# Nine convolution taps a tile by ScalarE and adding transfers, and two gate tiles taken out of a merge pair, in a hybrid decoder layer

## The chip, the cores and the metric

The kernel runs on one core of a Trainium2 chip, as one program in one launch. The metric is the device time of one execution in microseconds (us). The engines are named as the profile names them: PE is the matrix engine (TensorE), PEld its weight loads, DVE is VectorE, ACT is ScalarE, POOL is GpSimd, SP is the engine that issues most loads. DMA transfers issued from POOL can add what they carry onto what lies at their destination ("adding" or accumulating transfers); those from SP only copy.

## The reference

One layer over 512 tokens of 1,024 channels, all in float32. After a norm, one wide projection feeds two mixers that run side by side. Their outputs are gated, added and projected; a feed-forward block follows. Cut to what matters here:

```python
u = _rmsnorm(h, norm1_g[l])
proj = u @ w_in[l]
a_glu, q, k, v, r, g_low, gate_a, gate_b = _split_cols(proj)

c = a_glu[..., :CONV_CH] * jax.nn.sigmoid(a_glu[..., CONV_CH:])
c = _causal_dwconv(c, conv_dw_w[l], conv_dw_b[l])      # 31 taps for each channel
c = jax.nn.silu(_layernorm(c, conv_ln_g[l], conv_ln_b[l]))
y_conv = c @ w_conv_out[l]
...
o = _gla_chunked(qh, kh, vh, gkh)                      # 4 heads, chunks of 64 tokens
o = o * lax.rsqrt(jnp.mean(o * o, axis=-1, keepdims=True) + EPS) * gla_norm_g[l]
o = o.reshape(bsz, seq, GLA_VDIM) * jax.nn.silu(r)
y_gla = o @ w_gla_out[l]

merged = jax.nn.sigmoid(gate_a) * y_conv + jax.nn.sigmoid(gate_b) * y_gla
h = h + merged @ w_o[l]
u2 = _rmsnorm(h, norm2_g[l])
z = _causal_dwconv(u2 @ w_ffn_up[l], ffn_dw_w[l], ffn_dw_b[l])
h = h + (jax.nn.silu(z[..., :FFN_DIM]) * z[..., FFN_DIM:]) @ w_ffn_down[l]
```

## The kernel before

**Matrix products.** Each float32 operand is split into a high part, rounded to PE's reduced float32, and a low part, the rest. A product is three matmuls (`mm3`, L471: high by low, low by high, high by high). A weight tile is 128 by 1,024 values, 512 KB. `split_weight` (L368) makes the parts: ACT casts the high part (L380, L410); the low part comes from a DVE subtraction (L381, L415), or, for tiles in `ADDED` (L46), from a negated copy by ACT (L412) onto which a transfer from POOL adds the weight once more (L413). A plain tile (`col_tile`, L479) is 24 matmuls of 512 columns. `two_tiles` (L1211) computes two tiles together by seven products instead of eight, as 84 matmuls of 256 columns, with four weight splits, of sums that POOL adds up, and some combining operations.

**The stages.** (1) The first norm and half of v. (2) The glu tiles: for each of eight channel tiles one product for the gate, whose sigmoid ACT makes (L846), and one for the value, which DVE multiplies in (L850). (3) The low-rank decay (`w_low`), the other half of v (four accumulator banks at once, L501), the four heads' decays. (4) The heads: for each, queries, keys, scores, states and outputs, with other tiles between so that PE has work while DVE prepares. Three of the eight glu pairs stand here (`LATE_GLU`, L39), and after the last head four gb tiles (gate B), `AHEAD` of them. (5) `w_r`, the gate r, by a seven-product scheme over pairs. (6) The merge: six pairs of gate tiles (`MERGE`, L37), with the tiles of `w_gla` and `w_conv` between them (`BEHIND`). (7) `w_o` and the feed-forward block.

**The depthwise convolution.** It runs on DVE as background work. `conv_chain` (L801) turns a channel tile's 31 taps into two half-length sequences, 16 offsets with three operations each: one into the first half of `conv[k]`, one into its second half with the tap sums and x0 + x1 (L807), one into the tile's half of `aside`. Offset 0 is three activations on ACT (L811); offsets 1 to 15 are 44 operations on DVE (L815), each multiplying by a tap and adding; three closing operations follow (L829, L831, L833). When all eight tiles are through, `add_up` (L863) sums them for the layer norm's mean, and `norm_chain` does the rest.

**What sets the order.** Every use of a weight tile calls `weight` (L433), which prefetches the splits of the next two tiles and then calls `fill` (L455) with a share of work: `fill` pops operations from the first chain in `chains`, each costing 0.6 of room, until the room is used up. So the taps are dealt out along the weight tiles by a rate written by hand (`RATE`, the shares at L438). A new chain is appended by each glu pair (L851). The remaining order within an engine is made when the program is built and is fixed from then on: each engine runs its instructions strictly in that order, and waits at each for the semaphores that it needs. The buffers that matter: 5 PSUM banks `mm` and 3 `ax`, taken in turn; 4 raw weight tiles, 4 high and 4 low parts; 26 `h` tiles; `btmp` has 2 buffers, and one of them holds the tap sums as long as the convolution runs; `tmp` has 6.

Of the kernel before, what the change touches and what calls it, by code (L numbers as in the profile page):

```python
# [21 lines left out]
KT = D // P  # L22
# [12 lines left out]
AHEAD = 4  # L35

MERGE = [("w_gb", 4, 5), ("w_gb", 6, 7), ("w_ga", 0, 1), ("w_ga", 2, 3), ("w_ga", 4, 5), ("w_ga", 6, 7)]  # L37
R_PAIRS = ((0, 4), (1, 5), (2, 6), (3, 7))
LATE_GLU = 3  # L39
_HALVES = [("w_gla", 2 + h // 2, h % 2) for h in range(12)]  # L40
BEHIND = [[], _HALVES[:4], _HALVES[4:8], _HALVES[8:]]
BEHIND += [[("w_conv", m, half) for m in pair for half in range(2)] for pair in O_PAIRS[:2]]
MERGE_REST = [("w_conv", m) for pair in O_PAIRS[2:] for m in pair]
LOOK = 2
# [3 lines left out]
RATE = 5.0  # L48
WARM = (6, 1, 2, 2)
# [25 lines left out]
PP_N = PP_FB + 2 * FT  # L75


@with_exitstack
def trunk_layer(ctx: ExitStack, tc: tile.TileContext, a: dict, out: bass.AP):
# [139 lines left out]
    for h in range(HEADS):  # L219
        order += [("w_qk", 2 * h), ("w_qk", 2 * h + 1)]  # L220
        if h:
            order += glu_order[KT - LATE_GLU + h - 1]
# [4 lines left out]
    for (name, p, q), behind in zip(MERGE, BEHIND):  # L227
# [3 lines left out]
        if not behind:  # L231
            order += [("w_gla", 0), ("w_gla", 1)]
# [200 lines left out]
    def weight(name, j, ahead=LOOK):  # L433
# [5 lines left out]
        if name == "w_qk":  # L439
            share = 1.0 if j < 2 else RATE + 1.0  # L440

# [5 lines left out]
    room = [0.0]  # L447
    after, urgent, hold, conv_given = [], [], [True], []
# [5 lines left out]

    def fill(n):  # L455
        room[0] += n
        while (urgent or chains) and room[0] > 0:
            chain = urgent or chains[0]
            share, work = chain.pop(0)
# [5 lines left out]
            if chains and not chains[0]:  # L465
                chains.pop(0)
                start_chain()
# [333 lines left out]
    def conv_chain(k, c):  # L801
# [33 lines left out]
        chain = [(0.6, begin)]  # L835
        for j in range(ET_):
            for i in range(3 if j < OT_ else 2):
                chain.append((0.6 if j else 0, lambda j=j, i=i: list(parts(j))[i]()))
        return chain + [(0.6, lambda n=n: finish(n)) for n in range(3)]
# [295 lines left out]
    gbs = {}  # L1135

    def gate_b(m):
        gbs[m] = col_tile(weight("w_gb", m), acts1)
# [133 lines left out]
    for h in range(HEADS + 1):  # L1272
        old = heads[h - 1] if h else None
        new = heads[h] if h < HEADS else None
        if new:
            late_glu = glu(KT - LATE_GLU + h - 1)
            new.decays()
            new.queries()
        else:
            gate_b(0)  # L1280
# [4 lines left out]
        new.keys() if new else gate_b(1)  # L1285
        if old:
            old.states()
            next(late_glu) if new else gate_b(2)
            old.outputs()
            next(late_glu) if new else gate_b(3)  # L1290
# [6 lines left out]
    part = [None] * KT  # L1297
    gas = {}

    def sigmoid(m, acc):  # L1300
        g = heap()
        nc.scalar.activation(g, acc, AF.Sigmoid)
        return g
# [20 lines left out]

    for m in range(AHEAD):
        part[m] = sigmoid(m, gbs.pop(m))
# [118 lines left out]
    def pair_7(n):  # L1445
# [5 lines left out]
        for j in range(4):  # L1451
# [11 lines left out]
            if j == 0 or n >= 3:  # L1463
# [3 lines left out]
            if j == 3:  # L1467
# [7 lines left out]
                if n >= 3:  # L1475
# [15 lines left out]
    for n in range(4):  # L1491
# [384 lines left out]
```

## Time and profile before

| | us |
|---|---|
| median of 3 runs | 832.7 |
| the runs | 832.09, 832.7, 836.29 |
| the profiled execution | 833.33 |
| its span in the trace | 831.6 |

PE's granted clock in the profiled execution is 0.996 of full speed. A profile's page gives busy time by engine, and groups of instructions by source line ("L815 DVE ... x120 | 57.0, 475": 120 instructions, 57.0 us busy in all, 475 ns for one). "Waits" lists who waited for whom. A view by stretches gives the busy time of each engine between two times, and a timeline gives single instructions: start, duration, engine, line, output and inputs, and in brackets the idle time before it and what ended it. Instructions on one engine overlap at their ends, so the distance of starts tells what one costs, and a duration alone tells more than that. Transfers are listed with their size and the median time from issue to landing.

### The profile page before, as it was taken

To read this page: it belongs to the slowest core of one execution; us is meant where nothing else is said; L and a number is where in the kernel's file an instruction comes from. 1 tells how busy PE (TensorE), PEld (TensorE's weight loads), DVE (VectorE), ACT (ScalarE), POOL (GpSimd) and SP (SyncE) were. 2 spreads that over 40 slices of the span, in tenths; PEclk is the share of its full clock that TensorE was granted. 3 is DMA by queue.
4 is the path that set the end of the run, shared out by engine and by line. 5 is a ranking of instruction groups with operands and counts; after the bars stand their busy time and mean duration, and the time that the engine had idled before them with its cause. 6 is when DMAs were issued, how large, how long until landed. Compare 5 with 4: busy or idle time off the path is not lost.

```text
span 831.6 us, 11495 instructions
## 1 busy us (share of the span) xinstructions
PE 811.6 (98%) x4263; PEld 696.9 (84%) x4263; DVE 725.3 (87%) x1166; ACT 464.1 (56%) x688; POOL 167.9 (20%) x149
## 2 busy tenths in 40 slices
PE   9999999999989898999999999999999999999996
PEld 7888888887877777999988898899889988899885
DVE  6789999999998998676778889989974999789895
ACT  6654685746545544485444546556444663456654
POOL 2011111211122333323000200221122301522012
PEclk9999999999999999999999999999999999999999
DMA  8497868468213122334448633046643356334662
GB/s 327 141 200 180 233 148 199 107 157 201 52 50 96 63 96 76 102 102 153 129 125 227 178 102 102 26 130 176 144 133 102 107 172 151 116 102 164 166 127 101
DMA packets 36473, 113.60 MB, mean 137 GB/s; under 512 B 3689, under 2 KB 8945, under 8 KB 36417
## 3 DMA queue, kind: packets, MB, share of 16 engines
q1 hardware_dynamic: 28912, 86.39, 30.2%
q0 software_dynamic: 7488, 26.48, 18.6%
q8 instruction: 33, 0.54, 0.3%
q14 instruction: 24, 0.19, 0.1%
q10 hardware_dynamic: 16, 0.00, 0.0%
HBM read 110.76 MB, written 2.10 MB: 136 GB/s over the span
## 4 chain that ended last, share of the span: by engine, by line
PE 84%; DVE 10%; issue 3%; ACT 1%; DMA 0%; POOL 0%; POOLq 0%; DVEq 0%; ACTq 0%; SPq 0%
PE mm L475 24%; PE mm L476 24%; PE mm L477 24%; PE mm L689 3%; DVE wlo L381 2%; PE ax L477 2%; PE ax L476 2%; PE ax L475 2%; DVE c L815 2%; DVE aside L815 1%; DVE tmpq L1174 1%; DVE h L1431 1%; DVE wlo L415 1%; DVE btmp L869 1%; DVE kept L328 1%
## 5 line engine op out<-in xcount | busy, mean ns | idle before, releaser
L475 PE MATMUL mm<-uh,wlo 128*128 128x512 f32 (+1 forms) x608 | 219.7, 361 | 0.0
L476 PE MATMUL mm<-ul,whi 128*128 128x512 f32 (+1 forms) x608 | 217.5, 358 | 0.0
L477 PE MATMUL mm<-uh,whi 128*128 128x512 f32 (+1 forms) x608 | 217.2, 357 | 0.0
L477 PEld LDWEIGHTS mm<-uh,whi 128*128 128x128 f32 x608 | 114.8, 189 | 16.9
L475 PEld LDWEIGHTS mm<-uh,wlo 128*128 128x128 f32 x608 | 114.9, 189 | 16.7 <-issue 0.2
L476 PEld LDWEIGHTS mm<-ul,whi 128*128 128x128 f32 x608 | 114.9, 189 | 16.2
L381 DVE TENSOR_TENSOR wlo<-raw,whi 128x1024 fp32r<-128x1024 f32 x86 | 100.7, 1176 | 31.9 <-ACT whi L380 28.0
L352 POOL TENSOR_TENSOR raw<-raw,raw 128x512 f32<-128x512 f32 x42 | 65.1, 1551 | 249.3 <-DVE wlo L381 139.7
L380 ACT CAST whi<-raw 128x1024 fp32r<-128x1024 f32 x86 | 82.7, 964 | 38.3 <-PE mm L477 31.7
L410 ACT CAST whi<-raw 128x1024 fp32r<-128x1024 f32 x78 | 81.4, 1047 | 28.5 <-PE mm L477 13.1
L415 DVE TENSOR_TENSOR wlo<-raw,whi 128x1024 fp32r<-128x1024 f32 x50 | 66.6, 1336 | 7.6 <-ACT whi L410 7.3
L380 ACT CAST whi<-kept 128x1024 fp32r<-128x1024 f32 (+1 forms) x40 | 40.2, 1008 | 39.8 <-DVE kept L328 23.4
L815 DVE SCALAR_TENSOR_TENSOR c<-h,pp,c 128x255 f32<-128x255 f32 (+14 forms) x120 | 57.0, 475 | 1.6 <-ACT c L811 1.5
L815 DVE SCALAR_TENSOR_TENSOR c<-aside,btmp,c 128x255 f32<-128x255 f32 (+14 forms) x120 | 57.0, 475 | 0.0
L815 DVE SCALAR_TENSOR_TENSOR aside<-h,pp,aside 128x255 f32<-128x255 f32 (+6 forms) x112 | 53.2, 475 | 0.0
L381 DVE TENSOR_TENSOR wlo<-kept,whi 128x1024 fp32r<-128x1024 f32 (+1 forms) x40 | 47.8, 1195 | 5.0 <-ACT whi L380 4.9
L412 ACT ACTIVATE wlo<-raw 128x1024 fp32r<-128x1024 f32 x28 | 29.6, 1058 | 38.4 <-PE mm L475 29.4
L1600 DVE SCALAR_TENSOR_TENSOR tmp<-mm,pp,tmp 128x511 f32<-128x511 f32 (+1 forms) x56 | 41.3, 740 | 4.0 <-ACT tmp L1597 3.9
L1218 ACT COPY tmp<-mm 128x256 f32<-128x256 f32 x48 | 17.7, 368 | 43.7 <-PE mm L477 43.2
L1379 DVE TENSOR_TENSOR hres<-hres,mm 128x512 f32<-128x512 f32 (+1 forms) x49 | 32.2, 668 | 3.3 <-PE mm L477 2.4
L1597 ACT ACTIVATE tmp<-mm,pp 128x512 f32<-128x512 f32 x28 | 21.8, 777 | 19.1 <-PE mm L477 18.9
L352 POOL TENSOR_TENSOR raw<-raw 128x512 f32<-128x512 f32 x14 | 28.7, 2049 | 0.0
(383 smaller groups left out, 1902.9 us busy)
## 6 DMA issues: line engine op xcount, KB each, us to landing
raw<-in_w_up_dram SPq DMA_DIRECT2D x44, 512.0 KB, 3.6
raw<-in_w_glu_dram SPq DMA_DIRECT2D x16, 512.0 KB, 5.4
raw<-in_w_down_dram SPq DMA_DIRECT2D x15, 512.0 KB, 4.1
wlo<-in_w_glu_dram POOLq DMA_DIRECT2D x12, 512.0 KB, 6.8
kept<-in_w_down_dram POOLq DMA_DIRECT2D x10, 512.0 KB, 5.5
raw<-in_w_v_dram SPq DMA_DIRECT2D x8, 512.0 KB, 7.0
raw<-in_w_qk_dram SPq DMA_DIRECT2D x8, 512.0 KB, 7.2
wlo<-in_w_qk_dram POOLq DMA_DIRECT2D x8, 512.0 KB, 8.6
```

The source lines that it names most:

```text
L352: work = nc.gpsimd.tensor_tensor(out, x, y, ALU.add)
L380: nc.scalar.copy(hi, raw)
L381: two_low[:] = [nc.vector.tensor_tensor(lo, raw, hi.bitcast(F32), ALU.subtract)]
L410: nc.scalar.copy(hi, raw)
L412: pace[0] = nc.scalar.mul(lo, raw, -1.0)
L415: pace[0] = nc.vector.tensor_tensor(lo, raw, hi.bitcast(F32), ALU.subtract)
L475: nc.tensor.matmul(acc, ll, rh, start=first, stop=False, **kw)
L476: nc.tensor.matmul(acc, lh, rl, start=False, stop=False, **kw)
L477: nc.tensor.matmul(acc, lh, rh, start=False, stop=last, **kw)
L815: nc.vector.scalar_tensor_tensor(out[:, j:], x[:, : half_t - j], w, out[:, j:], ALU.mult, ALU.add)
L1379: done = nc.vector.tensor_tensor(hres[t, n][:, c], hres[t, n][:, c], acc[:, c], op)
L1600: nc.vector.scalar_tensor_tensor(z[:, s:], acc[:, : T - s], w[j], z[:, s:], ALU.mult, ALU.add)
```

## The change

1. `Taps`, a new kind of chain: its first three offsets (1, 2 and 3; tile 0 has none) can be done ahead by ACT and two adding transfers, as `added(j)`: three activations make the three products of an offset, two of them into one `btmp` tile and one into a `tmp` tile; then one transfer adds the `btmp` tile onto both halves of `conv[k]`, another the `tmp` tile onto `aside`. Each seventh time that `fill` takes an operation from the first chain, the second chain in the list starts its next one (`run_ahead`): first its offset 0, then an offset each time. What has not been started by the time that a chain comes to the front is done by DVE as before (`begin`).
2. `LATE_GLU` is 2: six glu pairs run in a row, two between the heads. In the place of the third stand two gb tiles; after the last head come four more. `AHEAD` is 6, and the pair gb 4 and 5 leaves `MERGE`.
3. `w_gla` tiles 6 and 7 are plain tiles behind the third pair, which had been halves behind the fourth; the sigmoids of gb tiles are taken at once; shares for the last gb tiles.

In the program as built, tile 1 has two offsets done ahead, tiles 2 to 5 have three each, tiles 6 and 7 none: 14 offsets, 42 operations that leave DVE, 42 activations and 28 transfers that come.

```diff
--- before.py
+++ after.py
@@ -32,20 +32,23 @@
 EPS = 1e-6
 O_PAIRS = ((0, 2), (1, 3), (4, 6), (5, 7))
 GROUPS = (((0, 2), (1, 3), (4, 6), (5, 7)), ((8, 10), (9, 11), (20, 21)), ((12, 14), (13, 15), (16, 18), (17, 19)))
-AHEAD = 4
-
-MERGE = [("w_gb", 4, 5), ("w_gb", 6, 7), ("w_ga", 0, 1), ("w_ga", 2, 3), ("w_ga", 4, 5), ("w_ga", 6, 7)]
+AHEAD = 6
+
+MERGE = [("w_gb", 6, 7), ("w_ga", 0, 1), ("w_ga", 2, 3), ("w_ga", 4, 5), ("w_ga", 6, 7)]
 R_PAIRS = ((0, 4), (1, 5), (2, 6), (3, 7))
-LATE_GLU = 3
-_HALVES = [("w_gla", 2 + h // 2, h % 2) for h in range(12)]
-BEHIND = [[], _HALVES[:4], _HALVES[4:8], _HALVES[8:]]
+LATE_GLU = 2
+_HALVES = [("w_gla", 2 + h // 2, h % 2) for h in range(8)]
+BEHIND = [[], _HALVES[:4], _HALVES[4:8]]
 BEHIND += [[("w_conv", m, half) for m in pair for half in range(2)] for pair in O_PAIRS[:2]]
 MERGE_REST = [("w_conv", m) for pair in O_PAIRS[2:] for m in pair]
+PLAIN_GLA = {0: (0, 1), 2: (6, 7)}
 LOOK = 2
 ADDED = {("w_glu", j) for j in range(4, 2 * KT)} | {("w_qk", m) for m in range(KT)}
 ADDED |= {("w_v", KT // 2 + j) for j in range(KT // 2)} | {("w_gb", m) for m in range(AHEAD)}
 RATE = 5.0
+TAPS_AHEAD = 3
+AHEAD_EVERY = 7
 WARM = (6, 1, 2, 2)
 MID = 4
 EARLY = 2
@@ -73,6 +76,21 @@
 PP_FW = PP_GG + DV // P
 PP_FB = PP_FW + 2 * FT * FW
 PP_N = PP_FB + 2 * FT
+
+
+class Taps(list):
+
+    def __init__(self, ahead, rest, taps):
+        super().__init__(rest)
+        self.ahead, self.taps = ahead, taps
+
+    def begin(self):
+        if self.ahead:
+            if len(self.ahead) == len(self.taps) + 1:
+                self.ahead.pop(0)()
+            at = len(self.taps) - len(self.ahead)
+            self[:0] = sum(self.taps[at:], [])
+            self.ahead = []
 @with_exitstack
@@ -218,18 +236,18 @@
     order += [("w_v", KT // 2 + j) for j in range(KT // 2)]
     for h in range(HEADS):
         order += [("w_qk", 2 * h), ("w_qk", 2 * h + 1)]
-        if h:
+        if 0 < h <= LATE_GLU:
             order += glu_order[KT - LATE_GLU + h - 1]
     order += [("w_gb", m) for m in range(AHEAD)]
     order += [("w_r", (R_PAIRS, step, d)) for step, d in R_STEPS]
     tight = set()
     first = len(order)
-    for (name, p, q), behind in zip(MERGE, BEHIND):
+    for n_pair, ((name, p, q), behind) in enumerate(zip(MERGE, BEHIND)):
         for n, part in enumerate(("x1", "x3", "x2", "x4")):
             order.append(("two", (name, p, q, part)))
             order += [tile[:2] for tile in behind[n : n + 1] if tile[2] == 0]
-        if not behind:
-            order += [("w_gla", 0), ("w_gla", 1)]
+        if n_pair in PLAIN_GLA:
+            order += [("w_gla", m) for m in PLAIN_GLA[n_pair]]
     tight |= set(range(first, len(order)))
     order += MERGE_REST
     order += [("w_o", (O_PAIRS, step, d)) for step, d in STEPS]
@@ -438,6 +456,8 @@
         share = {"two": 2.5, "w_glu": RATE + 0.75, "w_r": 2.0}.get(name, RATE)
         if name == "w_qk":
             share = 1.0 if j < 2 else RATE + 1.0
+        if name == "w_gb" and j > 3:
+            share = 2.0 if j == 4 else 6.8
         fill(share + (1.75 if order[min(len(ready), len(order)) - 1] in ADDED else 0))
         return ready[used[0] - 1]
@@ -445,17 +465,28 @@
     chains = []
     room = [0.0]
+    turn = [0]
     after, urgent, hold, conv_given = [], [], [True], []
     behind = []
     def start_chain():
         if not chains and after and conv_given == KT * [1] and not (hold and len(after) == 1):
             chains.append(after.pop()())
+
+    def run_ahead(chain):
+
+        turn[0] += 1
+        follower = chains[1] if len(chains) > 1 else None
+        if follower and follower.ahead and turn[0] % AHEAD_EVERY == 1:
+            follower.ahead.pop(0)()
     def fill(n):
         room[0] += n
         while (urgent or chains) and room[0] > 0:
             chain = urgent or chains[0]
+            if not urgent and isinstance(chain, Taps):
+                chain.begin()
+                run_ahead(chain)
             share, work = chain.pop(0)
             room[0] -= share
             with ExitStack() as order_of:
@@ -464,6 +495,7 @@
                 work()
             if chains and not chains[0]:
                 chains.pop(0)
+                turn[0] = 0
                 start_chain()
         if not chains and not urgent:
             room[0] = 0.0
@@ -832,11 +864,34 @@
             if n == 2:
                 nc.vector.tensor_tensor(y0[:, 1:], y0[:, 1:], other[:, : half_t - 1], ALU.add)
-        chain = [(0.6, begin)]
-        for j in range(ET_):
-            for i in range(3 if j < OT_ else 2):
-                chain.append((0.6 if j else 0, lambda j=j, i=i: list(parts(j))[i]()))
-        return chain + [(0.6, lambda n=n: finish(n)) for n in range(3)]
+        def start():
+            begin()
+            for part in parts(0):
+                part()
+
+        def added(j):
+
+            at = PP_CW + k * CW + CW - 1 - 2 * j
+            both = btmp().rearrange("p (two n) -> p two n", two=2)[:, :, : half_t - j]
+            odd = tmp(half_t)[:, : half_t - j]
+            src = slice(0, half_t - j)
+            for out, x, w in (
+                (both[:, 0], x0, pp[:, at : at + 1]),
+                (both[:, 1], xs, taps[:, k, j : j + 1]),
+                (odd, x1, pp[:, at - 1 : at]),
+            ):
+                nc.scalar.activation(out, x[:, src], AF.Copy, scale=w)
+            y = conv[k].rearrange("p (two n) -> p two n", two=2)[:, :, j:]
+            nc.gpsimd.dma_start(y, both, accum_op=ALU.add)
+            nc.gpsimd.dma_start(other[:, j:], odd, accum_op=ALU.add)
+
+        def by_dve(j):
+            return [(0.6, lambda i=i: list(parts(j))[i]()) for i in range(3 if j < OT_ else 2)]
+
+        ahead = range(1, 1 + TAPS_AHEAD if k else 1)
+        rest = sum((by_dve(j) for j in range(1, ET_) if j not in ahead), [])
+        rest += [(0.6, lambda n=n: finish(n)) for n in range(3)]
+        return Taps([start] + [lambda j=j: added(j) for j in ahead], rest, [by_dve(j) for j in ahead])
     sum_taps()
@@ -1132,10 +1187,15 @@
         low_at[:] = [nc.vector.scalar_tensor_tensor(lo, po, gain, hi.bitcast(F32), ALU.mult, ALU.subtract)]
         oa[m] = hi, lo
-    gbs = {}
+    part = [None] * KT
+
+    def sigmoid(m, acc):
+        g = heap()
+        nc.scalar.activation(g, acc, AF.Sigmoid)
+        return g
     def gate_b(m):
-        gbs[m] = col_tile(weight("w_gb", m), acts1)
+        part[m] = sigmoid(m, col_tile(weight("w_gb", m), acts1))
     H = T // 2
@@ -1273,34 +1333,28 @@
         old = heads[h - 1] if h else None
         new = heads[h] if h < HEADS else None
         if new:
-            late_glu = glu(KT - LATE_GLU + h - 1)
+            late_glu = glu(KT - LATE_GLU + h - 1) if h <= LATE_GLU else None
             new.decays()
             new.queries()
         else:
-            gate_b(0)
+            gate_b(2)
         if old:
             old.scores()
         if not new:
             urgent += s1_n2[:3] + of_s1 + s1_n2[3:] + of_n2
-        new.keys() if new else gate_b(1)
+        new.keys() if new else gate_b(3)
         if old:
             old.states()
-            next(late_glu) if new else gate_b(2)
+            next(late_glu) if h <= LATE_GLU else gate_b(0 if new else 4)
             old.outputs()
-            next(late_glu) if new else gate_b(3)
+            next(late_glu) if h <= LATE_GLU else gate_b(1 if new else 5)
     behind += [roots_at[0]]
     gla_scope.close()
     late_scope, late = scoped("late", 1, "right")
     r_scope, rp_ = scoped("r", 8, "right")
-    part = [None] * KT
     gas = {}
-
-    def sigmoid(m, acc):
-        g = heap()
-        nc.scalar.activation(g, acc, AF.Sigmoid)
-        return g
     def gla_out(m, py):
         nc.vector.tensor_tensor(part[m], py, part[m], ALU.mult)
@@ -1322,8 +1376,6 @@
             outs[name][1](m, acc[1])
         return acc
-    for m in range(AHEAD):
-        part[m] = sigmoid(m, gbs.pop(m))
     def seven(name, pairs, acts, complete, at=lambda step, i: None, fine=False, put=None, before=lambda step: None):
@@ -1460,7 +1512,7 @@
                     gated_o(m, ax_bank)
                 if j == 2:
                     start_norms()
-            if j == 0 or n >= 3:
+            if j == 0 or n >= 2:
                 while complete_pairs:
                     complete_pairs.pop(0)()
@@ -1472,7 +1524,7 @@
                         (part if name == "w_gb" else gas)[m] = sigmoid(m, c)
                 complete_pairs.append(sigmoids)
-                if n >= 3:
+                if n >= 2:
                     complete_pairs.pop()()
             for proj, m, half in behind[j : j + 1]:
                 open_tiles[proj, m] = tile_of(proj, m, half_of[half], open_tiles.get((proj, m)))
@@ -1488,17 +1540,16 @@
         hold.clear()
         start_chain()
-    for n in range(4):
+    for n in range(3):
         pair_7(n)
-        if n == 0:
-            for m in range(2):
-                tile_of("w_gla", m, range(KT))
+        for m in PLAIN_GLA.get(n, ()):
+            tile_of("w_gla", m, range(KT))
     def merged(m):
         if m not in merged_tiles:
             j = [m in p for p in O_PAIRS].index(True)
             if j < 2:
-                pair_7(4 + j)
+                pair_7(3 + j)
             else:
                 tile_of("w_conv", m, range(KT))
         return merged_tiles[m]
```

## The prediction

> **What bounds the kernel now.** I read the page's busy times first, then the waits of TensorE (PE), then busy time by stretch.
>
> ```profile
> span 831.6 us, 11495 instructions
> PE 811.6 (98%) x4263; PEld 696.9 (84%) x4263; DVE 725.3 (87%) x1166; ACT 464.1 (56%) x688; POOL 167.9 (20%) x149
> ```
>
> PE is short of the span by 20.0 us. No change that leaves PE's work alone can win more than that and whatever PE runs at a lower clock. The waits say where it is lost (us in total, times, longest):
>
> ```profile
> PE mm L475 <- DVE r L1429: 2.4, 1, 2.4
> PE ax L476 <- DVE wlo L381: 2.3, 1, 2.3
> PE mm L476 <- DVE wlo L381: 1.8, 2, 1.2
> PE mm L475 <- DVE wlo L415: 1.4, 2, 0.7
> PE ax L897 <- ACT sum L928: 1.2, 1, 1.2
> PE ax L897 <- DVE sum L929: 1.2, 1, 1.2
> PE ax L1124 <- DVE h L1132: 0.8, 1, 0.8
> ```
>
> All seven hang on VectorE (DVE) or on what stands just behind it; together 11.1 us. The stretches place them (stretch: length, then busy PE, weight loads, DVE, ScalarE (ACT), GpSimd (POOL), PE clock, DMA share, GB/s):
>
> ```profile
> 60.00:215.00 155.00, 154.80 (x704) 128.10 (x703) 152.04 (x372) 96.38 (x150) 25.68 (x28) 1.00 0.70 169
> 240.00:260.00 20.00, 15.86 (x68) 12.15 (x67) 20.00 (x29) 12.75 (x18) 6.93 (x4) 1.00 0.08 27
> 260.00:280.00 20.00, 17.57 (x78) 14.27 (x77) 17.36 (x19) 9.91 (x13) 5.11 (x3) 1.00 0.44 133
> 280.00:300.00 20.00, 18.39 (x136) 16.79 (x134) 20.00 (x37) 11.37 (x19) 1.38 (x1) 1.00 0.31 105
> 300.00:320.00 20.00, 17.06 (x76) 13.74 (x77) 19.64 (x23) 8.87 (x12) 7.60 (x4) 0.91 0.27 89
> 215.00:320.00 105.00, 93.77 (x461) 76.91 (x460) 101.60 (x146) 55.37 (x87) 24.00 (x14) 0.98 0.27 82
> 320.00:475.00 155.00, 155.00 (x878) 136.47 (x877) 115.79 (x156) 81.44 (x121) 33.63 (x25) 1.00 0.47 138
> ```
>
> From 240 to 320 us PE is idle 4.14 + 2.43 + 1.61 + 2.94 = 11.1 us: the same 11.1. That is the w_r product and the first merge pair, and DVE is full there (101.6 of 105). From 60 to 215 us (glu, w_v, the heads) DVE is full too, 152.0 of 155, and PE does not wait yet: the two are level. Behind 320 us PE never waits. One more loss shows in the clock of 0.91 after the last wait:
>
> ```profile
> 317.39 0.63 PE L476 MATMUL mm<-oa,whi 128*128 128x512 f32 x1
> 317.82 0.63 PE L477 MATMUL mm<-oa,whi 128*128 128x512 f32 x1
> ...
> 91.14 0.39 PE L475 MATMUL mm<-whi,ul 128*128 128x512 f32 x1
> ...
> 93.86 0.39 PE L475 MATMUL mm<-whi,ul 128*128 128x512 f32 x1
> ...
> 347.16 0.28 PE L476 MATMUL mm<-hq,whi 128*128 128x256 f32 x1
> 347.28 0.28 PE L477 MATMUL mm<-sumsq,whi 128*128 128x256 f32 x1
> ```
>
> Starts of 512-column matmuls are 0.43 us apart there, against 0.227 at 91 us (twelve steps in 2.72); the clock of 0.91 over 20 us says 1.8 us lost, and I count 1.6 (eight matmuls, 0.2 each). So 12.7 us hang on a late DVE behind 240 us.
>
> **The change, part by part.** *Matmuls.* Two gb tiles become plain tiles instead of a pair of seven products. By the changed order 84 matmuls of 256 columns go (x 0.12, the last pair of rows, = 10.1 us) and 48 of 512 come (x 0.227 = 10.9): +0.8 us of PE.
>
> *DVE behind 240 us.* In the changed order every tap of the last tile, and all additions of `add_up`, stand ahead of `of_s1`'s subtraction (L1187); before, 44 taps and these stood behind it.
>
> ```profile
> 87.76 0.47 DVE L815 SCALAR_TENSOR_TENSOR c<-aside,btmp,c 128x254 f32<-128x254 f32 x1
> 88.15 0.46 DVE L815 SCALAR_TENSOR_TENSOR aside<-h,pp,aside 128x254 f32<-128x254 f32 x1
> ...
> 89.34 1.11 DVE L850 TENSOR_TENSOR h<-mm,tmp 128x512 f32<-128x512 f32 x1
> ...
> L869 DVE TENSOR_TENSOR btmp<-btmp,c 128x512 f32<-128x512 f32 x6 | 6.2, 1030 | 0.1
> L866 DVE TENSOR_TENSOR btmp<-c,c 128x512 f32<-128x512 f32 x1 | 1.1, 1121 | 0.0
> ```
>
> A tap follows the last after 0.39 us: 44 are 17.2 us, `add_up` 7.3, the three closing operations 1.1. The gb pair's four splits and three combines go as well (about 5). From 215 to 320 us that is 31 of 101.6, and the 70 left are well under PE's 93.8. I let the waits go except the 0.8 at L1124, which stands directly behind w_r's last product, a real dependency: -11.9 us. If all goes it is -12.7.
>
> *DVE ahead of it.* The 25.6 us just named move into the glu and head stretch, less 42 taps that ScalarE takes over (14 offsets of three, for tiles 1 to 5: 16.4 us): +9.2 us of DVE there, against 10.9 more of PE (the two gb tiles) and 3.0 of idle DVE. Level again, with 4.7 to spare. Tiles 6 and 7 have nobody ahead of them and keep all their taps.
>
> *The new waits.* An offset now costs three activations, then two accumulating transfers from POOL, and of `btmp`'s two buffers one holds the tap sums throughout. So the next offset's first activation into `btmp` waits in ACT's own order until the last transfer has landed, and everything behind it on ACT waits too: weight casts, the negated copies, glu's sigmoids. POOL's second transfer into `aside` also waits for the first, ahead of weight transfers. And DVE can start the next tile only when its last offset has landed.
>
> ```profile
> 43.73 1.06 ACT L412 ACTIVATE wlo<-raw 128x1024 fp32r<-128x1024 f32 x1 [1.53 <-PE mm L475]
> 45.10 0.87 POOL L413 DMA_DIRECT2D wlo<-in_w_glu_dram  x1 [4.37 <-ACT wlo L412]
> ...
> 57.30 0.60 ACT L811 ACTIVATE c<-h,pp 128x256 f32<-128x256 f32 x1 [0.69 <-DVE h L850]
> 57.81 0.49 ACT L811 ACTIVATE aside<-h,pp 128x256 f32<-128x256 f32 x1
> ...
> wlo<-in_w_glu_dram POOLq DMA_DIRECT2D x12, 512.0 KB, 6.8
> wlo<-in_w_qk_dram POOLq DMA_DIRECT2D x8, 512.0 KB, 8.6
> raw<-in_w_down_dram POOLq DMA_DIRECT2D x5, 512.0 KB, 5.3
> raw<-in_w_down_dram POOLq DMA_DIRECT2D x1, 256.0 KB, 3.6
> ```
>
> One round t: two activations (1.0), from ACT's end to POOL's issue 0.3 (44.79 to 45.10), and the landing of 255 KB. Landing: from below 3.6 (256 KB of such a transfer, no load); from above 6.8 (512 KB among the glu loads). Halving saves 1.7 (5.3 to 3.6), so 5.1 under load. I take 4.6, nearer to the loaded row because the DMA share is 0.70 here: t = 5.9, with ends of 4.9 and 8.1. The other thing that would add, smaller pieces (1,020 bytes a row instead of 4,096), no row shows.
>
> Rounds against the DVE work that covers them, counted in the changed order from a tile's x0 + x1 (L807) to its first own tap into c: tile 1, two rounds, 18 taps, a glu product (1.1), three closing operations = 9.2 us; tile 2, three rounds, 32 taps and the same = 14.7; tile 3, three rounds, 35 taps, a glu product and small work = 16.8; tiles 4 and 5, three rounds, 20 and 22, because the gate's and the first head's operations stand between. Nothing before this slows DVE, so its lateness adds up to 8t - 40.7. What is late next is glu's sixth product (L850), which frees the fourth accumulator bank of w_v. Before, the last such product ended at 90.45 (89.34 + 1.11) and PE wanted the bank nine matmuls after w_v's first at 91.14, at 93.2: 2.7 to spare. In the changed order 23 more taps, a product and four small operations (11.5 us) stand ahead of it against two more glu tiles (10.9), so 2.1 are left. PE's wait = 8t - 42.8: at 5.9, **4.4 us**; at 4.9 nothing; at 8.1, 22.
>
> ACT's 42 activations (23 us at 0.55) and POOL's 28 issues (24 at 0.87) fit: ACT has 58 us and POOL 129 free from 60 to 215. The load order on SP changes by two gb tiles only and stays ahead. Behind 320 us one merge pair fewer stands between the layer norm and its use; DVE has 39 us of idle time there to cover it, so nothing.
>
> The Trainium skill ("DMA: Bandwidth & Descriptors", Anatomy of one DMA) puts a GpSimd transfer at 2.0 us plus bytes over 436 GB/s, an estimate of 2.6 for 255 KB; t would be 3.9 and the sum that of the first rival. Its 3.2 for 512 KB stands against 5.3 and 6.8 here, so I don't follow it.
>
> **Sum**, against the profiled execution (833.33 us with what lies around its 831.6 of span; the median of the runs shown is 0.6 lower): 833.3 - 11.9 + 0.8 + 4.4 = 826.6; against the median **826 us**.
>
> **Rivals.**
> *All landings are hidden* (t under 5.35). For it: the unloaded row. Against it: the DMA share of 0.70. 833.3 - 11.9 + 0.8 - 0.6 = 822 us.
>
> *The landings chain becomes the bound, and it is slower.* Place: ACT waiting for `btmp` in the glu stretch, seen by PE at w_low and w_v. It takes back the whole gain when 8t - 42.8 passes 11.1, at t = 6.7. Price: landing 5.1, activations 1.0, hand-over 0.3, one other transfer's issue in front 0.9: t = 7.3; 8t - 42.8 = 15.6, and tile 4 adds 3t - 20 = 1.9: 833.3 - 11.9 + 0.8 + 17.5 - 0.6 = 839 us. For it: qk's 8.6 to land. Against it: the loaded rows are of 512 KB, twice the size, and the unloaded one lands in 3.6. By the Trainium skill ("TensorE: Matmul & The Clock Gate", Part 1) PE drops to half clock after an idle window of some 3.4 us, which would put about 2 more on such a wait; the rows at 317 us show half speed after two waits of 1.2.
>
> *The change doesn't do what it says:* w_r's waits stay, because they hang on loads and not on taps.
>
> ```profile
> L328 DVE TENSOR_TENSOR kept<-kept,raw 128x1024 f32<-128x1024 f32 x6 | 7.8, 1302 | 2.5 <-DMA raw<-in_w_r_dram 2.5
> ```
>
> Then 2.4 + 2.3 + 1.8 remain: 833.3 - 5.4 + 0.8 + 4.4 - 0.6 = 832.5 us. Against it: DVE was busy 20.0 of 20 where PE lost most.
>
> **How the numbers follow.** Forecast 0.33, hidden 0.27, slower 0.27, doing nothing 0.13. Half a per cent, about what a measurement here can tell, is 4.2 us. Faster (under 828.5): all of hidden and three quarters of the forecast, 0.52. Slower (over 836.9): most of the slower rival, 0.26. Between: 0.22. The range must reach both: from 818 (hidden, with the last 0.8 and some of the rest of PE's small losses gone) to 840 (the slower rival); the forecast's own is 822 to 831.
>
> **What would show it.** Right: no taps behind L1187's first row and PE near 100% from w_r to the layer norm's mean; PE 0.8 us busier in matmuls; a PE gap of 2 to 8 us at w_low or w_v, with ACT waiting for a transfer out of `btmp`. Wrong: no gap there (822), a gap over 11 us or a second one at the heads (839), or PE still waiting for L381 or L1429 in w_r (832.5).

## The result and the profile after

| | before | after |
|---|---|---|
| median, us | 833.09 (4 runs, 832.09 to 836.29) | 876.55 (4 runs, 875.08 to 877.57) |
| ratio | | 1.0513, 95% interval 1.0481 to 1.0546 |
| span of the profiled execution | 831.6 | 874.6 |
| PE busy in it | 811.6 | 825.2 |
| span less PE busy | 20.0 | 49.4 |

The changed kernel is 43.5 us slower. Line numbers are now those of the changed kernel: L475 has become L507, L815 L847, L807 L839, L850 L905, L413 L431, L1429 L1481; new are the activations of L883 and the two adding transfers of L885 (into `c`) and L886 (into `aside`).

The page of after, first part:

```profile
span 874.6 us, 11483 instructions
PE 825.2 (94%) x4227; PEld 705.3 (81%) x4227; DVE 703.8 (80%) x1117; ACT 481.4 (55%) x726; POOL 190.7 (22%) x175
```

Every engine but PE has about the busy time that was expected; DVE has 21.5 us less. Busy time of after by stretch (columns as in the same view of before):

```profile
60.00:215.00 155.00, 116.76 (x444) 92.87 (x444) 102.46 (x247) 78.88 (x127) 44.66 (x46) 0.85 0.78 158
215.00:320.00 105.00, 104.43 (x478) 86.36 (x476) 92.77 (x181) 63.13 (x113) 21.22 (x17) 1.00 0.45 108
320.00:475.00 155.00, 153.10 (x894) 135.17 (x893) 115.99 (x145) 86.72 (x125) 34.40 (x22) 1.00 0.35 116
```

The first row is the loss: PE 38.2 short of 155 where it had been level, DVE at 102 where it had been at 152, and a clock of 0.85. No engine is near full there; they wait for one another. The second and third row hold the gain, though not in the same places as before, since everything stands later now (the wait for `r`, at 276.6 before, is at 336.0). PE's waits behind 200 us add up to 2.3 in after, and to 11.1 before. The waits of PE in after:

```profile
PE ax L1121 <- DVE k L1115: 7.6, 1, 7.6
PE mm L1022 <- ACT whi L409: 7.3, 1, 7.3
PE mm L507 <- ACT whi L428: 5.7, 1, 5.7
PE mm L507 <- DMA wlo<-in_w_qk_dram: 5.3, 2, 4.0
PE mm L507 <- DVE h L905: 5.2, 1, 5.2
PE mm L507 <- DMA wlo<-in_w_glu_dram: 3.9, 1, 3.9
PE ax L1036 <- DVE h L1027: 3.2, 1, 3.2
...
PE mm L507 <- DVE r L1481: 0.9, 1, 0.9
...
PE ax L1179 <- DVE h L1187: 0.3, 1, 0.3
```

The first seven, 38.2 us, are all new and lie between 90 and 200 us: glu, `w_low` (L1022), `w_v` (L905 frees its fourth bank), the decays (L1036), the first head's keys and scores (L1121). Of the old seven, two are left: `r` at L1481 with 0.9, and the one behind `w_r`'s last product (now L1179) with 0.3. Behind the new ones stand ACT's and DVE's own waits, in their fixed orders, for the new transfers:

```profile
ACT btmp L883 <- DMA c<-btmp: 54.1, 12, 8.1
DVE aside L847 <- DMA aside<-tmp: 16.4, 3, 8.1
DVE c L847 <- DMA c<-btmp: 14.7, 3, 7.3
```

DVE's six waits for landings are all in tiles 1 to 3, and add up to 31.1 us. The wait at the first head comes through ACT instead, which stands at tile 5's last offset ahead of the head's exponentials (L1087):

```profile
184.80 0.51 ACT L883 ACTIVATE btmp<-h,pp 128x253 f32<-128x253 f32 x1 [6.57 <-DMA c<-btmp]
...
187.02 0.63 ACT L1087 ACTIVATE tmp<-b 128x512 f32<-128x512 f32 x1
...
187.68 0.17 DVE L1096 TENSOR_TENSOR dec<-tmp 128x4 f32<-128x4 f32 x1 [11.99 <-ACT tmp L1087]
```

The waits are dear twice over. PE's timeline in after, around the wait at `w_low`:

```profile
104.00 0.39 PE L509 MATMUL mm<-uh,whi 128*128 128x512 f32 x1
111.72 0.79 PE L1022 MATMUL mm<-ul,whi 128*128 128x512 f32 x1 [7.33 <-ACT whi L409]
112.31 0.63 PE L1023 MATMUL mm<-uh,whi 128*128 128x512 f32 x1
...
117.01 0.63 PE L1022 MATMUL mm<-ul,whi 128*128 128x512 f32 x1
117.43 0.51 PE L1023 MATMUL mm<-uh,whi 128*128 128x512 f32 x1
```

From 112.31 to 117.43 twelve starts are 0.43 us apart instead of 0.227: 2.4 us more, on top of 7.3. The same distance of starts stands behind each of the seven waits of 3.2 us and more. The Trainium skill ("TensorE: Matmul & The Clock Gate", Part 1) has the half clock follow an idle window of about 3.4 us. The trace agrees here, behind a wait of 7.3. The traces don't give a threshold: half speed also follows two waits of 1.2 us (the prediction's rows at 317 us), and behind the wait of 1.4 us in after (the second for `w_qk`) the starts are 0.227 apart.

How long did a round take? DVE's timeline in after: x0 + x1 of tiles 1, 2 and 3 (L839), and the first tap of each that had to wait for its last landing (L847):

```profile
57.95 0.42 DVE L839 TENSOR_TENSOR aside<-h 128x256 f32<-128x256 f32 x1
...
76.15 0.48 DVE L847 SCALAR_TENSOR_TENSOR c<-h,pp,c 128x253 f32<-128x253 f32 x1 [0.16 <-DMA c<-btmp]
...
78.12 0.42 DVE L839 TENSOR_TENSOR aside<-h 128x256 f32<-128x256 f32 x1
...
92.97 0.42 DVE L839 TENSOR_TENSOR aside<-h 128x256 f32<-128x256 f32 x1
...
101.00 0.48 DVE L847 SCALAR_TENSOR_TENSOR c<-h,pp,c 128x252 f32<-128x252 f32 x1 [7.28 <-DMA c<-btmp]
...
131.86 0.48 DVE L847 SCALAR_TENSOR_TENSOR c<-h,pp,c 128x252 f32<-128x252 f32 x1 [7.27 <-DMA c<-btmp]
```

18.2 us for two rounds (tile 1) and 22.9 for three (tile 2). Tile 3's x0 + x1 stands in DVE's order ahead of the wait for tile 2's last landing, so its three rounds are counted from that landing, from 101.00 to 131.86: 30.9. That is 72.0 us for eight, t = 9.0, where the forecast had 5.9. The landing itself is the smaller part of the difference; the answer for L885 in after says

```profile
DMA to landing us min/median/max: 3.7/4.0/9.0
```

and the mean over tiles 1 to 3 is 5.3, where 4.6 was taken. The other 3.7 of a round lie between one landing and the next issue, where 1.3 was taken.

### The profile page after: what moved, and what is told of

Read it like the earlier page. It is cut to its first block, busy times and chain, and to the rows that moved or that the text cites. A ratio compares the mean times of both kernels' runs of the same rounds, so it can differ in the third digit from the quotient of the medians.

```text
span 874.6 us, 11483 instructions
## 1 busy us (share of the span) xinstructions
PE 825.2 (94%) x4227; PEld 705.3 (81%) x4227; DVE 703.8 (80%) x1117; ACT 481.4 (55%) x726; POOL 190.7 (22%) x175
## 4 chain that ended last, share of the span: by engine, by line
PE 76%; DMA 7%; issue 5%; DVE 5%; ACT 4%; POOL 2%; POOLq 0%; SPq 0%; ACTq 0%; DVEq 0%
PE mm L507 21%; PE mm L508 21%; PE mm L509 21%; DMA c<-btmp 5%; PE mm L721 3%; PE ax L509 2%; PE ax L508 2%; PE ax L507 2%; DVE c L847 2%; DMA raw<-in_w_v_dram 1%; DMA aside<-tmp 1%; POOL wlo L431 1%; DVE aside L847 1%; POOL aside L886 1%; ACT wlo L430 1%
## 5 line engine op out<-in xcount | busy, mean ns | idle before, releaser
L507 PE MATMUL mm<-uh,wlo 128*128 128x512 f32 (+1 forms) x612 | 225.0, 368 | 10.0 <-DMA wlo<-in_w_qk_dram 5.3
L508 PE MATMUL mm<-ul,whi 128*128 128x512 f32 (+1 forms) x612 | 222.3, 363 | 0.0
L509 PE MATMUL mm<-uh,whi 128*128 128x512 f32 (+1 forms) x612 | 221.6, 362 | 0.0
L507 PEld LDWEIGHTS mm<-uh,wlo 128*128 128x128 f32 x612 | 116.7, 191 | 29.4 <-issue 6.1
L399 DVE TENSOR_TENSOR wlo<-raw,whi 128x1024 fp32r<-128x1024 f32 x82 | 97.2, 1191 | 32.1 <-ACT whi L398 28.3
L370 POOL TENSOR_TENSOR raw<-raw,raw 128x512 f32<-128x512 f32 x39 | 59.5, 1525 | 238.2 <-DVE wlo L399 105.2
L428 ACT CAST whi<-raw 128x1024 fp32r<-128x1024 f32 x80 | 83.5, 1046 | 29.3 <-PE mm L509 15.4
L433 DVE TENSOR_TENSOR wlo<-raw,whi 128x1024 fp32r<-128x1024 f32 x50 | 66.4, 1333 | 7.3 <-ACT whi L428 7.1
L847 DVE SCALAR_TENSOR_TENSOR c<-h,pp,c 128x252 f32<-128x252 f32 (+14 forms) x106 | 50.5, 477 | 19.8 <-DMA c<-btmp 14.7
L847 DVE SCALAR_TENSOR_TENSOR aside<-h,pp,aside 128x251 f32<-128x251 f32 (+12 forms) x98 | 46.7, 477 | 16.5 <-DMA aside<-tmp 16.4
L847 DVE SCALAR_TENSOR_TENSOR c<-aside,btmp,c 128x252 f32<-128x252 f32 (+14 forms) x106 | 50.5, 477 | 0.1
L883 ACT ACTIVATE btmp<-h,pp 128x255 f32<-128x255 f32 (+2 forms) x14 | 7.1, 507 | 54.1 <-DMA c<-btmp 54.1
L507 PE MATMUL mm<-whi,ul 128*128 128x512 f32 x48 | 21.6, 450 | 11.7 <-ACT whi L428 5.7
```

The costliest lines, as they stand in the source:

```text
L370: work = nc.gpsimd.tensor_tensor(out, x, y, ALU.add)
L399: two_low[:] = [nc.vector.tensor_tensor(lo, raw, hi.bitcast(F32), ALU.subtract)]
L428: nc.scalar.copy(hi, raw)
L433: pace[0] = nc.vector.tensor_tensor(lo, raw, hi.bitcast(F32), ALU.subtract)
L507: nc.tensor.matmul(acc, ll, rh, start=first, stop=False, **kw)
L508: nc.tensor.matmul(acc, lh, rl, start=False, stop=False, **kw)
```

## The experiments

Times are medians; the ratio is to the kernel before, run beside each on the same chip, with its 95% interval. The span less PE busy is called PE's idle time.

**1. Room for POOL's transfers.** POOL's timeline in after:

```profile
60.07 1.21 POOL L885 DMA_DIRECT2D c<-btmp  x1 [3.41 <-ACT btmp L883]
63.20 0.91 POOL L886 DMA_DIRECT2D aside<-tmp  x1 [1.91 <-ACT whi L428]
64.60 0.87 POOL L431 DMA_DIRECT2D wlo<-in_w_glu_dram  x1 [0.49 <-issue]
67.77 0.86 POOL L886 DMA_DIRECT2D aside<-tmp  x1 [2.30 <-ACT whi L428]
72.25 1.18 POOL L885 DMA_DIRECT2D c<-btmp  x1 [3.62 <-issue]
```

The activations of tile 1's second offset ended at 65.3, and the transfer into `c` before it landed at 64.3, yet the second was issued at 72.25: 0.3 us after a weight's transfer (that of 64.60) had landed. It does not depend on that transfer.

```diff
-    nc = _bacc.Bacc("TRN2", ..., dynamic_dma_scratch_size=1024)
+    nc = _bacc.Bacc("TRN2", ..., dynamic_dma_scratch_size=2048)
```

> The changed kernel with dynamic_dma_scratch_size=2048 in place of 1024; no instruction changes. Theory S (space): POOL cannot issue a transfer until the ones in flight leave room; in the changed kernel most of the 28 added transfers start 0.3 us after some earlier transfer lands, also one they do not depend on, and never more than one other is in flight where a two-run transfer (c from btmp) is concerned. With twice the room those issues start when their own inputs are ready, the round between two transfers into c falls from 8 to 12 us to about 6, the PE waits of 38 us between 90 and 200 us fall under 15 and the time to 835 to 850. Theory L (landing): the rounds are long because the transfers themselves are slow under load; then nothing changes, 873 to 878. Theory Q (queue order): POOL's order, not its room, holds the issues back (each waits for the landing of the one before into the same tile); then under 5 us are won, 870 or more.

870.99 us, ratio 1.0456 (1.0422 to 1.0490): 5.6 won. POOL's timeline of this run:

```profile
60.21 1.20 POOL L885 DMA_DIRECT2D c<-btmp  x1 [3.43 <-ACT btmp L883]
60.94 1.41 POOL L886 DMA_DIRECT2D aside<-tmp  x1
61.63 1.63 POOL L431 DMA_DIRECT2D wlo<-in_w_glu_dram  x1
67.08 0.86 POOL L886 DMA_DIRECT2D aside<-tmp  x1 [3.82 <-ACT btmp L883]
67.66 1.49 POOL L885 DMA_DIRECT2D c<-btmp  x1
```

The issues now follow each other at once, as theory S had it: room was what they waited for. But it hardly paid. With more in flight the transfers into `c` of tiles 1 to 3 landed in 6.2 on average instead of 5.3, and t was 8.5. Most of the wait had moved from in front of the issue to behind it. S was right on the mechanism and wrong by 20 us and more on its worth; the time is in Q's range.

**2 to 4. Which half of the change, and a control.**

```diff
 (e2, the changed kernel)
-TAPS_AHEAD = 3
+TAPS_AHEAD = 0
```

e3 is the kernel before with the change's part 1 alone (`Taps`, `run_ahead`, `added`), which there has 11 offsets ahead instead of 14. e4, the control, is the kernel before with twice the room.

> The changed kernel with TAPS_AHEAD = 0: the new staging (two pairs of late glu tiles, two gb tiles between the heads, one merge pair fewer), and every tap on VectorE (ScalarE only the first of each tile, as before). Theory T (the loss is the taps ahead alone): no wait of PE for a transfer or for ScalarE's casts in the glu stretch; VectorE gets 16.4 us of taps back there and is late by about 12 us at the end of that stretch, so PE loses about 10 there and keeps the 11.9 won behind 240 us: 828 to 838. Theory R (the staging itself starves PE, by its order of loads and casts): 850 or more, with the waits at w_low, w_v and scores(0) still there.

828.66 us, ratio 0.9949 (0.9932 to 0.9965): faster than before, by 4.7, and in theory T's range. Its stretch of glu and heads:

```profile
60.00:215.00 155.00, 153.73 (x696) 127.64 (x695) 154.27 (x380) 97.73 (x145) 25.79 (x28) 1.00 0.72 171
```

DVE is full, 154.3 of 155, and yet PE loses only 1.3 there, not the 10 expected.

> The kernel before with the taps of ScalarE and the adding transfers put in, and its own staging kept (three late glu tiles, three merge pairs of seven products in w_r and w_gb). Theory T: the waits of PE at 90 to 200 us come with the taps, 25 to 45 us of them, and the 11 us behind 240 us mostly stay or shrink a little: 855 to 875. Theory R: without the new staging the taps cost nothing, 825 to 836.

867.65 us, ratio 1.0413 (1.0397 to 1.0428): theory T. The taps alone cost 34 us on the old staging (11 rounds) and 48 on the new one (14 rounds; 876.55 less 828.66).

> The kernel before with dynamic_dma_scratch_size=2048 in place of 1024, as a control. Theory S: there transfers from POOL stand at most three at a time and PE waits for none of them, so more room wins nothing: 831 to 835. If more room by itself made every transfer faster or slower, the time would leave that range.

834.03 us, ratio 1.0007 (0.9996 to 1.0017): without the new transfers, room changes nothing.

**5 and 6. Fewer rounds.** `TAPS_AHEAD = 1` and `TAPS_AHEAD = 2`.

> TAPS_AHEAD = 1: one offset of each of tiles 1 to 5 by ScalarE and transfer, five rounds in place of fourteen. Twice the room gave only 5 us back: the issues then started on time, but the transfers into c took 3.7 us alone and 5.3 to 7.5 behind a weight's transfer, so a round stayed at 8 to 9. Theory F: a round lasts about 8.5 us whatever holds it, because POOL's adding transfers share one queue with the weights', and three such rounds in a row do not fit under one tile of VectorE's work. By that t the order gives 7.6 + 10.7 + 8.3 + 7.2 + 5.6 = 39 us of lateness for three ahead (38 us of PE waits were measured). For one ahead the cover is 6.6, 14.6, 20.6, 21.5 and 28.1 us against one round each: 1.9 late in all, under the 2.1 of slack. So no PE wait for taps: 824 to 831. Rival G (a cost for every transfer, such as slowing loads or DVE): the loss is in proportion, 5 of 14 of the 47 us that taps cost over staging alone: 845.

833.17 us, ratio 1.0004 (0.9989 to 1.0019).

> TAPS_AHEAD = 2: two offsets each, ten rounds. Theory F: cover 9.4, 13.4, 17.0, 20.5 and 24.1 us against 17 each: 7.6 + 3.6 = 11 us late, 9 beyond the slack, some of it half clock: 832 to 840, the waits in the glu and w_v stretch only and none at the heads. Rival G: 10 of 14 of 47: 862.

854.42 us, ratio 1.0255 (1.0232 to 1.0278). The expectation for one ahead was wrong on the count: tiles 6 and 7 have an offset ahead too, and the trace shows seven transfers into `c`, not five. So 7 rounds cost 4.5 us over staging alone, 10 cost 25.8 and 14 cost 47.9. Rival G, a cost in proportion to the transfers, would give 24 for seven and is refuted by that run. Both times also lie above theory F's ranges, the second by 14 us and nearer to G's 862. Where F failed is seen in that second run: DVE waits 10.3 us for landings, about the 11 of F, but PE waits 16.5 us at the decays and the heads, where F had none.

**7. The activations without the transfers.**

```diff
-            nc.gpsimd.dma_start(y, both, accum_op=ALU.add)
-            nc.gpsimd.dma_start(other[:, j:], odd, accum_op=ALU.add)
```

> Both adding transfers of each offset left out; the activations stay, so the output lacks nine taps of five tiles. Theory F (the rounds are transfers; ScalarE's 42 activations fit): no wait behind them, PE like staging alone or better, 820 to 828. Rival H (ScalarE's own order: the activations delay its casts and sigmoids): PE waits for whi and wlo stay, 840 or more.

823.94 us, ratio 0.9892 (0.9872 to 0.9912). Its page:

```profile
span 821.9 us, 11405 instructions
PE 807.3 (98%) x4227; PEld 694.9 (85%) x4227; DVE 702.5 (85%) x1117; ACT 481.2 (59%) x726; POOL 160.7 (20%) x147
```

The output lacks the taps here, but the order of the rest is the same. ACT's 42 activations cost PE nothing; the whole loss is the transfers. This run splits it: after has 49.4 - 14.6 = 34.8 us more of PE's idle time, and 825.2 - 807.3 = 17.9 more of busy time in the same number of matmuls. 34.8 + 17.9 = 52.7, and the times differ by 52.6. Most of the 17.9 is the slow clock behind the seven longer waits: 1.7 to 2.9 us behind each, 16.0 together, by the distances of starts. The run also shows how late PE is at the place that the forecast named, `w_v`'s fourth bank (in after, then here):

```profile
133.37 0.79 PE L507 MATMUL mm<-whi,ul 128*128 128x512 f32 x1 [5.20 <-DVE h L905]
...
104.11 0.39 PE L507 MATMUL mm<-whi,ul 128*128 128x512 f32 x1
```

29.3 us later: 22.1 of waits and the slow clock behind them. The other 23.3 of the 52.6 come behind this place, at the decays and the heads.

**8 and 10. What a landing competes with.** e8 leaves out the weights' adding transfers of `w_glu`, `w_v` and `w_qk`:

```diff
-                pace[0] = nc.scalar.mul(lo, raw, -1.0)
-                nc.gpsimd.dma_start(lo, a[name][spec], accum_op=ALU.add)
+                if name == "w_gb":
+                    ...
+                else:
+                    pace[0] = nc.scalar.mul(lo, raw, 0.0)
```

> The adding transfers of the weights' low parts left out for w_glu, w_v and w_qk (the low part is written as zero by the same ScalarE instruction), all the taps' transfers kept: the output misses the low parts' products' share. Theory F: the transfers into c now land in 3.7 to 4.5 each and are issued when their inputs are ready, so t is 5 to 6 and my sum 8t - 42.8 gives 0 to 5 us: 822 to 834. Rival C (the rounds are long from ScalarE's order, DVE's order or the loads on SP's queue): t stays at 8 or more, 855 or more.

858.00 us, ratio 1.0301 (1.0281 to 1.0322), 18.6 less than after; t in tiles 1 to 3 was 6.9. The time is in rival C's range, t between the theories' two: the weights' transfers are about a third of the loss of 52.6 and not all of it. Part of the 18.6 is what PE itself waited for them in after (9.2). e10 also leaves out the second transfer of each offset (`aside`).

> As the kernel without the weights' adding transfers (858), and also without the second transfer of each offset, into aside; the output misses those taps and the low parts. Between the last landing of tile 1 and of tile 5 lie 12 rounds: 115.6 us in the changed kernel (9.6 each), 110.7 with twice the room, 96.0 without the weights' transfers (8.0). Theory P (transfers in flight together slow each other, 3.7 us alone against 5.7 to 7.4 beside another): without the sibling a round is 3.7 + 1.4 and a tile adds some 4 us from its last landing over VectorE's x0 + x1 to the next first issue: 77 us for the 12, near the 73.5 of cover that I counted: 826 to 838. Rival D (the loads on SP's queue, or ScalarE's order, hold a round): 12 rounds stay over 90 us and the time over 850.

848.36 us, ratio 1.0180 (1.0150 to 1.0210): theory P missed, and rival D met by the 12 rounds (90 us) and nearly by the time; t was 6.4 in tiles 1 to 3. What still held the rounds is seen in this run's timeline (POOL, ACT and SP's queue):

```profile
73.15 1.19 POOL L888 DMA_DIRECT2D c<-btmp  x1 [6.44 <-ACT btmp L886]
...
76.90 0.51 ACT L886 ACTIVATE btmp<-h,pp 128x254 f32<-128x254 f32 x1 [1.88 <-DMA c<-btmp]
...
78.24 1.22 POOL L888 DMA_DIRECT2D c<-btmp  x1 [3.89 <-ACT btmp L886]
78.77 0.33 SPq L284 DMA_DIRECT2D raw<-in_w_v_dram  x1
...
84.17 0.51 ACT L886 ACTIVATE btmp<-h,pp 128x253 f32<-128x253 f32 x1 [4.46 <-DMA c<-btmp]
```

Beside the transfer of 73.15 no other was under way, and it landed after 3.7; the one of 78.24 had a load of 512 KB half a microsecond behind it and took 5.9. Of the 14, nine landed in 3.6 to 3.9, and none of these shared more than 2 us with a load of 512 KB; five took 5.8 to 6.2, each with such loads beside it for 4 us or more.

**11. One transfer an offset.** ACT makes only the two taps of `c`; the third of each offset (into `aside`) goes back to DVE.

```diff
-                (odd, x1, pp[:, at - 1 : at]),
...
-            nc.gpsimd.dma_start(other[:, j:], odd, accum_op=ALU.add)
```

> Only the two taps that go into c are ScalarE's and one transfer's; the third of each offset (into aside) is VectorE's again, 14 taps or 5.5 us more on VectorE. Weights' transfers and the room of 1024 as in the changed kernel. Theory P: a round loses its sibling but still stands behind a weight's transfer: 12 rounds in 95 to 108 us, 852 to 868. Rival E (the second transfer alone makes the rounds long): 12 rounds under 80 us, 835 to 842.

857.61 us, ratio 1.0291 (1.0263 to 1.0319): theory P. The smaller transfer costs 19 us, although DVE has 5.5 us more to do without it. Without it DVE waits 7.8 us for landings instead of 31.1; 16.4 of those had been for `aside`. The 12 rounds still take 106 us against 115.6 in after, so rival E is refuted.

**12 to 14. Is it ScalarE's wait?** The pieces for `c` go to `tmp`, so that ACT has a buffer to write while the last transfer is under way; in e13 with twice the room, in e14 also with one offset ahead.

```diff
-            both = btmp().rearrange("p (two n) -> p two n", two=2)[:, :, : half_t - j]
+            both = tmp().rearrange("p (two n) -> p two n", two=2)[:, :, : half_t - j]
```

> The pieces for c are written to the six rotating buffers of tmp in place of the one free buffer of btmp, so ScalarE need not wait for a landing before it writes the next offset (it waits 54 us for c from btmp in the changed kernel). POOL still waits, since each transfer adds onto the tile that the last one added onto. Theory A (ScalarE's wait in its own order starves casts and sigmoids, and that is what PE feels): PE's waits for whi at L409 and L428 (7.3 and 5.7) and the hand-over between tiles go, 835 to 855. Theory K (the chain of landings sets VectorE's tiles, whoever waits): a round only loses ScalarE's 1.0 us, 14 us in all, and the waits come back at VectorE and at POOL: 855 to 868.

869.28 us, ratio 1.0426 (1.0389 to 1.0462). PE's waits in this run:

```profile
PE mm L507 <- DMA wlo<-in_w_qk_dram: 16.7, 2, 9.7
PE mm L507 <- DMA wlo<-in_w_glu_dram: 9.7, 2, 8.4
PE ax L1036 <- DVE h L1027: 7.7, 1, 7.7
PE mm L507 <- DVE h L905: 5.2, 1, 5.2
```

Theory K, a little over its range. The waits for ACT's casts (L409, L428) are gone, and the waits for weights' adding transfers are 26.4 us instead of 9.2: with ACT free, POOL is the one that stands still, and the weights stand behind its taps.

> The same with dynamic_dma_scratch_size=2048. Theory A: POOL issues each transfer as soon as the one before has landed, 830 to 848. Theory K: the transfers then run more together and slow one another as in the first run with twice the room, which gave 5.5 us: 848 to 864.

864.11 us, ratio 1.0372 (1.0344 to 1.0399). Theory K again, at the upper edge.

> One offset ahead, tmp buffers and twice the room: every wait found so far is taken away from a single round per tile. If the rounds were all that ate the relief of 15 taps (5.9 us), this is 824 to 829, at or under staging alone (828.7). If it stays at 832 or more, a single round costs VectorE's tile order as much as it saves.

830.11 us, ratio 0.9962 (0.9946 to 0.9979), between the two cases that were expected. e9, the same without the change of buffers:

> One offset ahead and the doubled room together. With one ahead four of the five transfers into c still started 0.3 us after some weight's transfer had landed, and VectorE's tiles finished no sooner than under staging alone (fifth tile 185.9 against 186.9 us), so 15 taps of relief were eaten by one round per tile. If that was the room, this gives the relief back: PE's waits at the heads (3.7 and 3.4) go, 825 to 830. If one round costs VectorE as much as three taps save whatever the room, it stays at 831 to 835. The bound from below is 823.9, the time with no adding transfers at all.

834.00 us, ratio 1.0007 (0.9994 to 1.0021): it stays, so room alone doesn't bring the relief. So with a buffer and room a single round per tile costs almost nothing (830.1 against 828.7 with none), but the taps that it takes over (21 with seven rounds, not the 15 that were expected) bring nothing either. Two things on record bear on that. There was little to win: with all 42 taps gone and no transfer (e7) the time is only 4.7 us below e2. And in e14 tile 7's transfer still isn't hidden (DVE, then PE):

```profile
210.28 0.48 DVE L847 SCALAR_TENSOR_TENSOR c<-h,pp,c 128x254 f32<-128x254 f32 x1 [3.71 <-DMA c<-tmp]
...
217.13 1.22 PE L1161 MATMUL ax<-state,q 128*128 128x256 f32 x2 [3.94 <-DVE state L1145]
```

e2 and e7 have no wait of PE at L1161. Both e14 and e2 beat the kernel before; no kernel here that does all the work beats the new staging with all its taps on DVE (e2).

## Why the prediction was wrong

826 us was forecast, 876.55 measured. The steps in their order:

- *Gain behind 240 us: -11.9.* Right for the most part: PE's waits behind 200 us fell from 11.1 to 2.3, where the forecast left 0.8, and the clock from 215 to 475 us is 1.00. In time it was worth less: 9.5 us where 42 taps are taken off DVE and no transfer stands in their place (e7, 833.49 before beside it), 4.7 by staging alone (e2).
- *Matmuls: +0.8.* Not seen: e7 does the new set of matmuls in 807.3 us of busy time against 811.6 before, and busy time also holds the slow clock, so a term of this size can't be told from it.
- *DVE's glu and head stretch level with PE, 4.7 to spare.* Right and not tight: e2, with 16.4 us more on DVE, loses 1.3 there.
- *ACT's activations and POOL's issues fit.* Right for ACT (e7). For POOL only as busy time.
- ***The new waits, one round t = 5.9 (ends 4.9 and 8.1).*** This step failed. t was 9.0, outside both ends. With it the prediction's own formulas hold: DVE late by 8t - 40.7 = 31.3 us, and its waits for landings are 31.1; PE late by 8t - 42.8 = 29.2 at `w_v`'s fourth bank, and it is 29.3 late there against e7. So the cover and the slack were sized right, the place was right (`w_low`, `w_v`, ACT waiting for `btmp`), and the price of one round was not. The landing was near (5.3 against 4.6; alone 3.6 to 3.9, also with pieces of 1,020 bytes, as for the 256 KB row that the prediction read). What was priced at 1.3 and took 3.7 was the way from a landing to the next issue, through ACT's and POOL's orders and POOL's room. Taking competitors away shows the size: e1, room, t 8.5; e8, no weights' transfers, 6.9; e10, no sibling either, 6.4.
- *Tiles 4 and 5, nothing.* They were taken as covered, which goes with the same step: three rounds at 5.9 are 17.7, under their cover of 20 and 22, and at 9.0 they are 27. In after PE waits 16.1 us behind `w_v`'s fourth bank up to the first head, against 3.6 in e7; the way there was through ACT's and POOL's orders, and DVE waits for no landing of these two tiles.
- *The slow clock: nothing in the forecast, "about 2" in a rival.* Busy time is 17.9 us longer, a third of the loss, nearly all of it behind the seven waits of over 3 us. The rule was cited, and counted for one wait.

The rivals: *hidden*, 822, is what e7 measures with no transfers at all, 823.9, so the bound was good and the condition (t under 5.35) out of reach even in e10. *The landings chain becomes the bound* is what happened, at the place named and with the second gap at the heads (L1121, 7.6); with t = 7.3 and no clock it gave 839. *The change does nothing for w_r* is refuted by after.

At short rounds the formula counts a little too little: with t = 6.9 and 6.4 it gives 12.4 and 8.1 us at `w_v`'s fourth bank, and e8 and e10 are 14.9 and 11.0 late there against e7. It says nothing of what comes behind. Of the 23.4 us of PE's idle time that e8 has more than e7, 12.1 are waits up to that bank, and most of the rest are waits at the heads (5.7 for the first head's keys, 4.6 at its query product). How much of the loss at the heads each of ACT's and POOL's orders makes stays open: e12, with ACT free, has no wait for the keys, and 16.7 instead of 5.3 for `w_qk`'s transfers.

## What to carry to other kernels

Price a hand-over between engines by the whole loop from one result to the next issue, through each in-order queue and what stands in it; a transfer's landing time is only a part of it (5.3 of 9.0 us here), and the part that was misjudged was the other one. Before moving work to transfers that add onto the same tile one after the other, count how many must follow in a row and compare with the work of one tile: one round a tile cost 4.5 us here (1.5 with a buffer and room), up to three in a row 48. Ask first what the relief is worth: here all 42 taps were worth 4.7 us (e7 against e2). When several longer waits are predicted on TensorE, add the slow clock behind each of them; behind each wait of over 3 us it was 1.7 to 2.9 us.

## What the runs showed of the hardware

- POOL's transfers have a limited room in flight. At `dynamic_dma_scratch_size=1024`, with a transfer of two runs a row (into `c`) never more than one other was in flight, while of plain ones (L413 before) three were seen together; several issues then started 0.3 us after some landing, and with 2048 they follow each other at once (e1). The profile names the idle time of POOL "issue" or puts it down to an engine that had long been done. The Trainium skill ("DMA: Bandwidth & Descriptors", SWDGE vs HWDGE vs iDMA) says that GpSimd appends descriptors to rings in a part of SBUF. That an issue waits for room, and that the program sets how much there is, is what these runs add.
- An adding transfer of 253 to 255 KB from SBUF to SBUF took 3.6 to 3.9 us alone, 5.8 to 6.2 beside a load of 512 KB, and up to 9.0 in after beside a load and a weight's adding transfer. The estimate of 2.6 that the prediction drew from the Trainium skill ("DMA: Bandwidth & Descriptors", Anatomy of one DMA) lies below every one of them.
